# Scaling of the differential heads behind blocks of the first merge branch, and pending differential products ahead of the last latent transposes

## The chip, the cores and the metric

One Trainium2 chip, one of its cores. The metric is the device time of the whole program in microseconds (us). The program is built with a tile framework that plans the order of the instructions on each engine: it simulates the run, and whenever an engine is free it gives it the ready instruction that stands first in the program text. So an instruction may overtake earlier ones of its engine, unless the kernel ties it down. Once planned, the order on an engine is fixed, and the engine waits wherever a real transfer is later than the simulated one.

## The reference

Two layers of an encoder over 512 tokens and 1024 channels, all float32:

```python
for l in range(DEPTH):                       # DEPTH = 2
    h = _rmsnorm(x, g_mix_pre[l])
    z = h @ w_in[l]                          # latents, q/k/v of two branches, 3 gates
    o_a = _mla(c_q, c_kv, k_r, ...)          # 8 heads, low-rank q and kv, rotary part
    o_b = _dilated(...)                      # 4 heads, 3 strided groups, relative bias
    o_c = _diff(...)                         # 4 heads, two softmax maps, RMSNorm of each head
    gates = sigmoid(gz)
    merged = (gates[:, :, 0] * (o_a @ w_branch[l, 0]) + gates[:, :, 1] * (o_b @ w_branch[l, 1])
              + gates[:, :, 2] * (o_c @ w_branch[l, 2]))
    x = x + _rmsnorm(merged @ w_out[l], g_mix_post[l])
    x = x + _rmsnorm(relu(_rmsnorm(x, ..) @ w_up[l]) ** 2 @ w_down[l], ..)
```

The RMSNorm of a differential head divides its output by the root mean square over its 128 channels, token by token. The kernel calls this step the scaling of the head.

## The kernel before, in words

Every dense product is made of three float32r matmuls: operands are split into a high part (`whi`, `hhi`, a rounding copy on ACT) and a low part (`wlo`, `hlo`, a subtraction on DVE, or on POOL where the text says so). A weight block of 128 x 1024 is loaded on SP's queue into `wraw` (4 buffers), split, and used by `mm3` (L132).

A layer goes through these stages in the text:

- The opening of the first layer: `x` is loaded in four blocks of 128 tokens; `norm_scale` normalises a block, and `norm_turn` transposes it on TensorE (`ntp`, into `hhi` and `hlo`). `head_start` computes four products (`zq`) on the first two token blocks while blocks 2 and 3 are still being normalised by `start`, called through `turns`.
- Dilated heads (`dil_head`), differential heads (`diff_head`), latents (`latent`, `latent_turn`: products `cp`, transposes `ctp`), then eight latent heads (`mla_head`). A head works in four rounds of 128 queries. A round makes scores (`s`, `sd`, `ms`), a softmax on DVE, ACT and POOL, and puts its transposes (`tp`) and, every second round, its product with the values (`do`, `fo`, `mo`) on the list `pending`. `tick(2)` runs the entries more than two rounds old, and `drain()` runs all of them. In a product of a differential head, L679 adds the squares (`sp`), and `ond` and `rdr` in HBM receive the unscaled head and its reciprocal roots.
- `fill(n)` hands TensorE n units of the 24 gate products (`gp`). A unit is 6 matmuls and a gate has 4 units, so a layer has 96; fractions are carried over in `owed`. The argument is `RATES` per round, 1.5 in dilated, 2.0 in differential and 1.0 in latent heads, with 2.0 and 1.75 in the first two latent heads and `fill(2.0)` ahead of the last latent transposes. `fill(1000)` finishes the gates.
- The merge: for branch 1 (dilated), 2 (differential), 0 (latent), eight products `bp` of 12 matmuls each, two to a weight block; the loaded gate `gl` multiplies each, and DVE adds it to `macc`. `bp` has two PSUM buffers (tag `mm`), so a third product waits for the `macc` of the first. In branch 2, `diff_norm` loads a head and its factors (`dn<-ond`, `dn<-rdr`), multiplies them on DVE and splits the result into `ot` on ACT and DVE.
- Output projection (`e`), and the MLP (`up`, `p`, `e`).

`InOrder` wraps an engine: while `on`, each instruction is tied behind the one traced before it on its engine. Tiles of one tag share buffers: `se` (6) holds `em`, `dn` and `xn`; `pair` (13) holds the values and `ot`; `gt` (2) holds gates and `gl`. Before the change the opening is tied on ACT, DVE and SP until `head_start` has been traced in full. The POOL copies `wk` behind the latents are tied to the POOL instruction traced before them.

Of the kernel before, what the change touches and what calls it, by code (L numbers as in the profile page):

```python
# [26 lines left out]
RATES = (1.5, 2.0, 1.0)  # L27
# [39 lines left out]
class InOrder:  # L67


    def __init__(self, tc, eng):  # L70
        self.tc, self.eng, self.on = tc, eng, False

    def __getattr__(self, name):
        fn = getattr(self.eng, name)

        def call(*args, **kw):
            ins = fn(*args, **kw)  # L77
            if self.on:
                self.tc.keep_in_program_order(ins)
            return ins  # L80

        return call
# [8 lines left out]
def _trunk(ctx, tc, nc, a):  # L91
# [6 lines left out]
    def in_order(on, engines=(act, vec, sync)):  # L98
        for e in engines:
            e.on = on  # L100
# [10 lines left out]
    def pair(name, dt=F32R):  # L111

        t = sb.tile([128, 2, 512], dt, name=name, tag="pair", bufs=13)
        return t[:, 0], t[:, 1]
# [13 lines left out]
    def f(x):  # L128
        return x.bitcast(F32)
# [58 lines left out]
    def split_w(raw, cols=1024, eng=None):  # L188
        hi = sb.tile([128, 1024], F32R, name="whi", tag="whi", bufs=4)
        lo = sb.tile([128, 1024], F32R, name="wlo", tag="wlo", bufs=4)  # L190
        act.activation(hi[:, :cols], raw[:, :cols], AF.Copy)
        (eng or vec).tensor_tensor(lo[:, :cols], raw[:, :cols], f(hi)[:, :cols], op=OP.subtract)
        return hi, lo
# [188 lines left out]
    def by_chunk(t):  # L382

        return t.rearrange("p (j q) -> p q j", q=4)
# [39 lines left out]
    def chunked(t):  # L424
        return t.rearrange("p (c j) -> p c j", c=4)
# [45 lines left out]
    otd = {}  # L471
# [34 lines left out]
    def layer(l, h, first_w):  # L506
# [18 lines left out]
        def fill(n):  # L525
            owed[0] += n
            while owed[0] >= 1.0:
                owed[0] -= 1.0
                if next(gates, "end") == "end":
                    return  # L530
# [34 lines left out]
        def dil_head(hd, q, k, v, rate):  # L565
            b = hd % 2
            bt = biases.pop(0)
            ahead = None

            def product(half, pt):  # L570
                o = pst("do", "o", 256)
                for c in range(4):
                    cs = slice(hd * 128, hd * 128 + 128)
                    mm3(o, v[c][0][:, cs], v[c][1][:, cs], pt[0][:, c], pt[1][:, c], c == 0, c == 3)
                hi = tmp("doh", F32R)
                lo = tmp("dol", F32R)
                act.activation(hi[:, :256], o, AF.Copy)
                vec.tensor_tensor(lo[:, :256], o, f(hi)[:, :256], op=OP.subtract)
                store_ot(1, hd, half, hi, lo)

            pts = {}
            for r in range(4):
                half, i = r // 2, r % 2
                s0, s1 = pst("s0", "s"), pst("s1", "s", 256)
                score(s0, q[0], k[0], b, r * 128, 0, 512)
                score(s1[:, 0:128], q[1], k[1], b, r * 128, r * 128, 128)
                score(s1[:, 128:256], q[2], k[2], b, r * 128, r * 128, 128)
                s = se("sd", 768)
                m = small("dm", 4)
                vec.tensor_tensor_reduce(out=s[:, :512], in0=s0, in1=bt[:, (3 - r) * 128:(7 - r) * 128],  # L590
                                         scale=1.0, scalar=-3e38, op0=OP.add, op1=OP.max,
                                         accum_out=m[:, 0:1])
                vec.tensor_tensor_reduce(out=s[:, 512:], in0=s1, in1=bt[:, 896:], scale=1.0, scalar=-3e38,
                                         op0=OP.add, op1=OP.max, accum_out=m[:, 1:2])
                vec.tensor_scalar(m[:, 2:3], m[:, 0:1], m[:, 1:2], -0.125, op0=OP.max, op1=OP.mult)
                act.activation(s, s, AF.Exp, bias=m[:, 2:3], scale=0.125, accum_out=m[:, 3:4])
                rc = small("dr")
                vec.reciprocal(rc, m[:, 3:4])
                blk = s[:, r * 128:(r + 1) * 128]
                pool.tensor_tensor(s[:, 512:640], s[:, 512:640], s[:, 640:768], op=OP.add)  # L600
                pool.tensor_tensor(blk, blk, s[:, 512:640], op=OP.add)
                act.activation(s[:, :512], s[:, :512], AF.Copy, scale=rc)
                if hd < 3 and r == 0:
                    ahead = dil_bias(hd + 1)
                    biases.append(next(ahead))
                if hd < 3 and r == 2:
                    next(ahead)
                if l == 0 and r % 2:
                    next(evens, None)

                def flip_p(s=s, half=half, i=i):
                    if i == 0:
                        pts[half] = new_pt()
                    transpose_p(s, pts[half], i, flip)

                pending.append((flip_p, (lambda half=half: product(half, pts[half])) if i else None))
                tick(LAGS[0])
                fill(rate)

        first_bias = dil_bias(0)  # L620
        biases = [next(first_bias)]
# [152 lines left out]
        for c in range(4):  # L774
            z, zp = latent(c), z
            if c:
                latent_turn(c - 1, zp)
        fill(2.0)
        latent_turn(3, z)
        vec.tensor_tensor(kr[0:32], kr[0:32], krs[0:32], op=OP.add)  # L780
        qe = [sb.tile([128, 2, 512], F32R, name=f"q{e}", tag="pair", bufs=13) for e in range(2)]
# [130 lines left out]
            vm.append(row)  # L912
        for hp in range(4):
            hold = []
            mla_head(2 * hp, hold, RATES[2] if hp else 2.0)
            if hp < 3:
                place = mla_prep(hp + 1)
                place(0)
            mla_head(2 * hp + 1, hold, RATES[2] if hp else 1.75)
            if hp < 3:  # L920
                place(1)
# [1 line left out]
        fill(1000)  # L923


        def diff_norm(hd, out):

            t = se("dn", 1024)
            o, rb = t[:, :512], t[:, 512:]
            sync.dma_start(o, ond[hd])  # L930
            sync.dma_start(rb, bass.AP(tensor=rdr.tensor, offset=rdr.offset + hd * 512, ap=[[0, 128], [1, 512]]))
            vec.tensor_tensor(chunked(o), chunked(o), by_chunk(rb), op=OP.mult)
            act.activation(out[0], o, AF.Copy)
            vec.tensor_tensor(out[1], o, f(out[0]), op=OP.subtract)

        macc = [None] * 8
        mh, ml = [None] * 8, [None] * 8
        for bi, b in enumerate((1, 2, 0)):
            ot = [pair("ot") for _ in range(4)]
            for kc in range(4):  # L940
                if b == 2:
                    diff_norm(kc, ot[kc])
                    continue
                for j in range(2):
                    sync.dma_start(f(ot[kc][j]), otd[b][kc, j])
            for dp in range(4):
                w = weights(wi("w_branch")[b * 4 + dp])
                hi = w[0].rearrange("p (d k n) -> p d k n", d=2, k=4)
                lo = w[1].rearrange("p (d k n) -> p d k n", d=2, k=4)
                for d2 in range(2):  # L950
                    d = dp * 2 + d2
                    t = sb.tile([128, 512], F32, name="gl", tag="gt", bufs=2)
                    sync.dma_start(t, gated[b, d])
                    p = mmt("bp")
                    for k4 in range(4):
                        mm3(p, hi[:, d2, k4], lo[:, d2, k4], ot[k4][0], ot[k4][1], k4 == 0, k4 == 3)
                    if bi == 0:
                        if d2 == 0:
                            mt = sb.tile([128, 2, 512], F32, name="macc", tag="pt", bufs=4)
                        macc[d] = mt[:, d2]  # L960
                        vec.scalar_tensor_tensor(macc[d], t, 1.0, p, op0=OP.add, op1=OP.mult)
                    else:
                        vec.scalar_tensor_tensor(t, t, 1.0, p, op0=OP.add, op1=OP.mult)
                        vec.tensor_tensor(macc[d], macc[d], t, op=OP.add)
                    if bi == 2:
                        mh[d], ml[d] = pair("mrg")
                        act.activation(mh[d], macc[d], AF.Copy, scale=0.5)
                        vec.scalar_tensor_tensor(ml[d], macc[d], 0.5, f(mh[d]), op0=OP.mult, op1=OP.subtract)


        gpost = load_g(wi("g_mix_post"), "gpost")
# [212 lines left out]
        for qd in range(4):  # L1184
# [32 lines left out]
            last = l == DEPTH - 1  # L1217
# [24 lines left out]
    def start(c):  # L1242
        xns[c] = norm_scale(xs[c], g0)
        norm_turn(xns[c], c, h)
# [28 lines left out]
    ws = [split_w(raws[0], eng=pool)]  # L1273
    norm_turn(xns[1], 1, h)
    ws.append(split_w(raws[1]))
    for c in range(2, 4):
        turns[c] = lambda c=c: start(c)
    first = list(head_start(blocks, h, turns, "zq", ws))
    sync.dma_start(flip, a["flip"])
    in_order(False)  # L1280
    setup_bias()
    got = []
    def all_setup():
# [102 lines left out]
```

## Time and profile before

| | |
|---|---|
| median of 3 runs | 1871.1 us (1870.99 to 1872.38) |
| profiled execution | 1869.85 us, span 1868.1 us |
| granted TensorE clock, mean | 0.998 |
| TensorE matmul busy | 1820.8 us (97% of the span) |
| DVE, ACT, POOL busy | 67%, 51%, 27% |

The span is what the profiler saw between the first and last instruction; the execution's own time has 1.75 us around it. All times in rows count from the span's start. A matmul's end is modelled and overlaps the next one, so a stretch of matmuls is best read from start to start, or as a piece of the chain of work.

### The profile page before, as it was taken

The page shows a single profiled execution, that of the slowest core. Times are in us where ns is not written, and L with a number is a line of the kernel's source. Part 1 is how long each engine was busy: PE and PEld are TensorE (multiplying, and loading weights), DVE is VectorE, ACT ScalarE, POOL GpSimd, SP SyncE. Part 2 cuts the span into 40 slices and gives each one's busy share as a digit, 9 for nine tenths or more (in the row PEclk, how much of TensorE's full clock was granted, in tenths as well). Part 3 has the DMA queues.
Part 4 walks back from the last instruction along what each step waited for, and adds up shares of the span by engine and source line. Part 5 has one row for each costly group of instructions (what it writes and reads, how often), then busy time and mean ns, then how long its engine had stood idle before and what let it go on. Part 6 is the DMA issues. An engine that isn't in the chain of part 4 may idle for free.

```text
span 1868.1 us, 24762 instructions
## 1 busy us (share of the span) xinstructions
PE 1820.8 (97%) x9002; PEld 1523.6 (82%) x9002; DVE 1260.3 (67%) x2024; ACT 960.7 (51%) x1605; POOL 499.1 (27%) x367
## 2 busy tenths in 40 slices
PE   7999999999999999999999999999999999999998
PEld 6788788888777988788888887888887888878886
DVE  4855376656677786888674455675667779587965
ACT  4466355478525453443554554554783354543433
POOL 1344212331000242347123222114200015241542
PEclk9999999999999999999999999999999999999999
DMA  4365554346675432424453333544468562414243
GB/s 161 104 210 195 178 186 136 101 142 194 233 239 204 146 100 81 135 68 149 148 194 107 118 119 119 156 152 121 139 211 276 181 225 68 156 47 152 70 162 136
DMA packets 105843, 281.13 MB, mean 150 GB/s; under 512 B 13470, under 2 KB 19942, under 8 KB 105719
## 3 DMA queue, kind: packets, MB, share of 16 engines
q1 hardware_dynamic: 105718, 279.53, 46.0%
q8 instruction: 71, 1.16, 0.3%
q14 instruction: 54, 0.43, 0.1%
HBM read 228.50 MB, written 39.96 MB: 144 GB/s over the span
## 4 chain that ended last, share of the span: by engine, by line
PE 64%; DVE 10%; issue 4%; POOL 4%; DMA 3%; ACT 2%; SPq 0%; POOLq 0%; DVEq 0%; ACTq 0%
PE up L132 12%; PE gp L132 12%; PE p L132 9%; PE zq L132 7%; PE e L132 5%; PE bp L132 3%; DVE fr L77 3%; DVE wlo L77 3%; PE ms L132 2%; PE tp L465 2%; PE cp L132 2%; PE sd L132 2%; PE mo L132 1%; DVE fs L77 1%; POOL fr L77 1%
## 5 line engine op out<-in xcount | busy, mean ns | idle before, releaser
L77 ACT ACTIVATE whi<-wraw 128x1024 fp32r<-128x1024 f32 (+1 forms) x270 | 283.9, 1054 | 274.6 <-PE up L132 52.8
L77 DVE TENSOR_TENSOR wlo<-wraw,whi 128x1024 fp32r<-128x1024 f32 (+1 forms) x213 | 274.8, 1293 | 142.7 <-ACT whi L77 141.3
L77 POOL TENSOR_TENSOR wlo<-wraw,whi 128x1024 fp32r<-128x1024 f32 x57 | 139.3, 2447 | 369.5 <-ACT whi L77 369.5
L132 PE MATMUL up<-hlo,whi 128*128 128x512 f32 (+1 forms) x576 | 210.4, 366 | 0.0
L132 PE MATMUL up<-hhi,wlo 128*128 128x512 f32 (+1 forms) x576 | 210.4, 366 | 0.0
L132 PE MATMUL up<-hhi,whi 128*128 128x512 f32 (+1 forms) x576 | 209.9, 366 | 0.5 <-ACT hhi L77 0.5
L132 PE MATMUL p<-whi,fs 128*128 128x512 f32 x672 | 208.0, 389 | 0.0
L77 POOL TENSOR_TENSOR dw<-dw 128x1024 f32<-128x1024 f32 x48 | 132.1, 2755 | 144.6 <-DVE wlo L77 143.6
L132 PE MATMUL gp<-hhi,whi 128*128 128x512 f32 x384 | 153.0, 398 | 1.9 <-DVE ql L77 1.9
L132 PE MATMUL gp<-hhi,wlo 128*128 128x512 f32 x384 | 150.8, 393 | 0.3 <-POOL wlo L77 0.3
L132 PE MATMUL gp<-hlo,whi 128*128 128x512 f32 x384 | 150.3, 391 | 0.0
L132 PEld LDWEIGHTS p<-whi,fs 128*128 128x128 f32 x672 | 126.1, 188 | 26.1
L77 DVE TENSOR_TENSOR wlo<-dw,whi 128x1024 fp32r<-128x1024 f32 x84 | 138.0, 1662 | 13.7 <-POOL fr L77 10.9
L132 PE MATMUL zq<-hhi,whi 128*128 128x512 f32 (+1 forms) x384 | 138.7, 364 | 5.5 <-DVE ql L77 2.6
L132 PE MATMUL zq<-hhi,wlo 128*128 128x512 f32 (+1 forms) x384 | 138.7, 362 | 1.7 <-DVE wlo L77 1.0
L132 PE MATMUL zq<-hlo,whi 128*128 128x512 f32 (+1 forms) x384 | 138.3, 361 | 1.7 <-DVE hlo L77 1.7
L132 PE MATMUL p<-wlo,fs 128*128 128x512 f32 x336 | 131.5, 391 | 2.6 <-DVE wlo L77 2.6
L132 PE MATMUL bp<-ot,whi 128*128 128x512 f32 x384 | 120.3, 392 | 4.8 <-DVE macc L77 3.9
L77 ACT ACTIVATE whi<-dw 128x1024 fp32r<-128x1024 f32 x84 | 88.1, 1058 | 68.4 <-PE p L132 42.9
L132 PEld LDWEIGHTS up<-hlo,whi 128*128 128x128 f32 x576 | 108.6, 189 | 17.9 <-DVE hlo L77 0.4
L132 PEld LDWEIGHTS up<-hhi,whi 128*128 128x128 f32 x576 | 108.1, 188 | 18.4 <-ACT hhi L77 1.0
L132 PEld LDWEIGHTS up<-hhi,wlo 128*128 128x128 f32 x576 | 108.6, 189 | 17.5
(257 smaller groups left out, 4053.7 us busy)
## 6 DMA issues: line engine op xcount, KB each, us to landing
wraw<-in_w_up_dram SPq DMA_DIRECT2D x64, 512.0 KB, 4.3
wraw<-in_w_gate_dram SPq DMA_DIRECT2D x48, 512.0 KB, 3.7
dw<-in_w_down_dram SPq DMA_DIRECT2D x48, 512.0 KB, 3.4
btd<-ddram SPq DMA_DIRECT2D x64, 256.0 KB, 3.3
wraw<-in_w_out_dram SPq DMA_DIRECT2D x32, 512.0 KB, 3.4
wraw<-in_w_down_dram SPq DMA_DIRECT2D x32, 512.0 KB, 3.5
wraw<-in_w_dil_dram SPq DMA_DIRECT2D x24, 512.0 KB, 4.7
gated<-gt SPq DMA_DIRECT2D x48, 256.0 KB, 3.0
```

Of the source, the lines that this page charges most:

```text
L77: ins = fn(*args, **kw)
L132: pe.matmul(out, lhsT, rhs, start=first, stop=last)
L465: pe.transpose(p[:, k * 128:(k + 1) * 128], e[:, k * 128:(k + 1) * 128], perm)
```

## The change

Five edits. `InOrder` remembers its last tied instruction. In each first dilated head, rounds 0 and 1 get one gate unit more. The `fill(2.0)` ahead of the last latent transposes becomes `drain()`, and the first latent head gets 2.25 units per round. `diff_norm` becomes a generator: its loads are traced ahead of the weights of branch 1, and its arithmetic, tied on ACT and DVE, after each pair of blocks of that branch. In the opening, the tie ends ahead of `head_start`; only `start(2)` and `start(3)` are still queued behind the last tied instructions of ACT and DVE.

```diff
@@ InOrder
+                self.last = ins.ins
@@ dil_head
-                fill(rate)
+                fill(rate + (1.0 if hd == 0 and r < 2 else 0.0))
@@ ahead of the last latent transposes
-        fill(2.0)
+        drain()
         latent_turn(3, z)
@@ latent heads
-            mla_head(2 * hp, hold, RATES[2] if hp else 2.0)
+            mla_head(2 * hp, hold, RATES[2] if hp else 2.25)
@@ merge
-        def diff_norm(hd, out):
+        def diff_norm(hd):
             t = se("dn", 1024)
             o, rb = t[:, :512], t[:, 512:]
             sync.dma_start(o, ond[hd])
             sync.dma_start(rb, bass.AP(tensor=rdr.tensor, offset=rdr.offset + hd * 512, ap=[[0, 128], [1, 512]]))
+            yield
+            out = pair("ot")
+            in_order(True, [act, vec])
             vec.tensor_tensor(chunked(o), chunked(o), by_chunk(rb), op=OP.mult)
             act.activation(out[0], o, AF.Copy)
             vec.tensor_tensor(out[1], o, f(out[0]), op=OP.subtract)
+            in_order(False, [act, vec])
+            yield out
...
         for bi, b in enumerate((1, 2, 0)):
-            ot = [pair("ot") for _ in range(4)]
-            for kc in range(4):
-                if b == 2:
-                    diff_norm(kc, ot[kc])
-                    continue
-                for j in range(2):
-                    sync.dma_start(f(ot[kc][j]), otd[b][kc, j])
+            if b == 2:
+                ot = normed
+            else:
+                ot = [pair("ot") for _ in range(4)]
+                for kc in range(4):
+                    for j in range(2):
+                        sync.dma_start(f(ot[kc][j]), otd[b][kc, j])
+            if b == 1:
+                norms = [diff_norm(kc) for kc in range(4)]
+                for n in norms:
+                    next(n)
+                normed = []
             for dp in range(4):
...
+                if b == 1:
+                    normed.append(next(norms[dp]))
@@ opening
     ws.append(split_w(raws[1]))
+    last = [act.last, vec.last]
+    in_order(False)
+
+    def later(c):
+
+        with tc.issue_after(last[0]), tc.issue_after(last[1]):
+            start(c)
+
     for c in range(2, 4):
-        turns[c] = lambda c=c: start(c)
+        turns[c] = lambda c=c: later(c)
     first = list(head_start(blocks, h, turns, "zq", ws))
     sync.dma_start(flip, a["flip"])
-    in_order(False)
```

## Rows read from the trace of the kernel before

**Rows 1.** The page: each engine's busy time, share of the span, and instructions.

```profile
PE 1820.8 (97%) x9002; PEld 1523.6 (82%) x9002; DVE 1260.3 (67%) x2024; ACT 960.7 (51%) x1605; POOL 499.1 (27%) x367
```

**Rows 2.** Waits of TensorE: waiter, awaited, us in total, times, longest.

```profile
PE bp L132 <- DVE macc L77: 3.9, 2, 3.0
PE ctp L762 <- DVE zc L77: 3.2, 2, 1.6
```

**Rows 3.** Timeline of TensorE, opening: start, us, instruction, [idle before, releaser].

```profile
30.55 0.38 PE L132 MATMUL zq<-hhi,whi 128*128 128x256 f32 x1 [1.68 <-ACT whi L77]
...
31.81 0.38 PE L132 MATMUL zq<-hhi,wlo 128*128 128x256 f32 x1 [0.76 <-DVE nst L77]
```

**Rows 4.** Timeline of SP, DVE and ACT, opening.

```profile
5.47 1.17 SPq L77 DMA_DIRECT2D wraw<-in_w_dil_dram  x2
...
15.82 0.21 DVE L77 TENSOR_SCALAR gds<-cols 128x1 f32<-128x1 f32 x2 [2.72 <-DMA cols<-in_cols_dram]
...
29.44 1.06 ACT L77 ACTIVATE whi<-wraw 128x1024 fp32r<-128x1024 f32 x1
```

**Rows 5.** Timeline of POOL and TensorE, first dilated heads of both layers.

```profile
85.88 8.09 POOL L77 TENSOR_TENSOR wlo<-wraw,whi 128x1024 fp32r<-128x1024 f32 x3 [17.55 <-ACT whi L77]
...
95.72 0.66 PE L465 MATMUL tp<-flip,sd 128*128 128x128 f32 x4 [1.70 <-ACT sd L77]
...
1016.18 0.55 PE L465 MATMUL tp<-flip,sd 128*128 128x128 f32 x3 [0.84 <-ACT sd L77]
```

**Rows 6.** Timeline of all engines, last latent block, first layer.

```profile
356.57 1.61 POOL L77 CAST wk<-whi 128x512 fp32r<-128x512 f32 x1
...
357.25 0.20 ACT L77 ACTIVATION_READ_ACCUMULATOR zc<-cp 128x1 f32 x1
...
358.83 1.31 POOL L77 TENSOR_SCALAR csv<-cst 128x1 f32<-128x1 f32 x2
...
361.49 0.59 PE L762 MATMUL ctp<-ident,zc 128*128 128x128 f32 x3 [1.61 <-DVE zc L77]
```

**Rows 7.** Timeline of ACT and DVE, the latent block before it.

```profile
351.96 0.20 ACT L77 ACTIVATION_READ_ACCUMULATOR zc<-cp 128x1 f32 x1
...
353.27 0.74 DVE L77 TENSOR_SCALAR zc<-cp,csr 128x256 f32<-128x256 f32 x2 [2.25 <-POOL csr L77]
```

**Rows 8.** Chain of work: start, us, what; a gate stretch and a product.

```profile
373.38 2.75 PE gp L132 x12
...
380.21 1.42 PE fo L132 x12
```

**Rows 9.** Timeline of TensorE: one round's transposes.

```profile
335.75 0.60 PE L465 MATMUL tp<-flip,ed 128*128 128x128 f32 x4
```

**Rows 10.** Timeline of SP, DVE and TensorE, merge of the first layer.

```profile
492.83 0.43 SPq L77 DMA_DIRECT2D dn<-rdr  x1
...
505.11 1.06 DVE L77 TENSOR_TENSOR dn<-dn 128x512 f32<-128x512 f32 x1 [2.61 <-DMA dn<-rdr]
...
508.56 0.73 PE L132 MATMUL bp<-ot,whi 128*128 128x512 f32 x2 [2.99 <-DVE macc L77]
```

**Rows 11.** Chain of work, merges of both layers: start, us, what.

```profile
498.34 6.74 DMA dn<-rdr
...
1426.40 46.54 PE bp L132 x204
```

**Rows 12.** Groups by form, 488 to 532 us: count | busy, mean ns | idle before.

```profile
L77 DVE TENSOR_TENSOR wlo<-wraw,whi 128x1024 fp32r<-128x1024 f32 x6 | 7.3, 1217 | 0.2 <-ACT whi L77 0.2
L77 DVE SCALAR_TENSOR_TENSOR macc<-gl,bp 128x512 f32<-128x512 f32 x8 | 5.4, 683 | 3.7 <-PE bp L132 3.6
L77 DVE TENSOR_TENSOR dn<-dn 128x512 f32<-128x512 f32 x4 | 4.3, 1076 | 3.1 <-DMA dn<-rdr 3.1
...
L77 DVE TENSOR_TENSOR ot<-dn,ot 128x512 fp32r<-128x512 f32 x4 | 2.8, 690 | 0.8 <-ACT ot L77 0.7
L77 ACT ACTIVATE ot<-dn 128x512 fp32r<-128x512 f32 x4 | 2.5, 632 | 10.3 <-DVE dn L77 7.8 <-DMA dn<-ond 2.5
```

More of the change, by code (lines that the diff above doesn't have):

```diff
@@ L70, in __init__ @@
     def __init__(self, tc, eng):
-        self.tc, self.eng, self.on = tc, eng, False
+        self.tc, self.eng, self.on, self.last = tc, eng, False, None
     def __getattr__(self, name):
```

## The prediction

> **What bounds the kernel now.** I read the shares on the page first: TensorE is busy 97% of the span, DVE 67%, ACT 51%, POOL 27% [rows 1]. So the sum of the matmuls is the bound, and none of the five edits takes a matmul away. What can be won is TensorE's idle time, some 47 us by these shares. The second view is the list of what TensorE waited for, the third the timeline at each place that an edit touches: there the reader is to see which engine is late, and what stands ahead of the late instruction on it. Four places count. In the opening the products wait for a weight split and then for DVE [rows 3]. In the first dilated head the first transposes wait for ACT, in both layers [rows 5]. The last latent transposes wait for DVE, once in each layer [rows 2, 6]. In the merge a product waits for `macc`, twice in all [rows 2, 10].
>
> The measurement tells about 0.2% from no change, here 3.7 us.
>
> **The opening.** The weight block 3 is loaded early: SP issued blocks 2 and 3 at 5.47 [rows 4]. Its split on ACT runs only at 29.44 [rows 4], since it is tied behind the copies of `norm_turn(2)`, which stands before it in the text. TensorE waits 1.68 us for it, and 0.76 us more on DVE's queue, 2.44 together [rows 3]. With the tie gone, block 3 can be split while TensorE still works on block 2, and the norm of block 3 of `x` goes ahead of it too; `start(2)` and `start(3)` stay behind the last tied split. Bounds: 2.44 gained if both waits go; nothing if the planner leaves the order, or if the second norm's transposes meet a new wait as long as 0.76. I take 2.44 less 0.3.
>
> **The first dilated head.** At its third round TensorE has no more to do until the first softmax is scaled: 1.70 us in the first layer, 0.84 in the second [rows 5]. The edit puts two gate units, 12 matmuls, ahead of that point. Twelve take 2.75 us [rows 8], more than either wait, so 2.54 goes. No matmul is added: the units come out of later rounds. The cover needs the next gate's weights in time, and POOL, which splits them, also does this softmax's additions: three splits take 8.09 us, 2.70 each [rows 5]. One more split ahead of the additions would cost up to 2.70 a layer, the lower bound. The three already run before the additions and reach past the units now asked for, so I take 2.54.
>
> **The last latent transposes.** TensorE does two gate units and then waits 1.61 us; the list of waits has two such, 3.2 us [rows 2, 6]. The last square sum is ready at 357.45, but POOL turns to it at 358.83, being held by the copies `wk` that started at 356.57 [rows 6]. A block earlier the same chain ran from 352.16 to 354.01, 1.85 us [rows 7]. By that the last block would be ready at 359.30, some 2 us before 361.49. `drain()` does two things. It puts the two open rounds of the last differential head into the hole: two groups of transposes of at most 0.60 each and two products of 1.42, 4.04 us, and two short stretches of `sp`, where the 2.75 of gate work and the wait make 4.36 [rows 6, 8, 9]. And the last POOL instruction traced before `wk` is now the reciprocal root of that head, so `wk` is tied behind it and no longer runs ahead of the latent chain. What is late next is the second product: it needs its transposes copied by ACT and subtracted by DVE, which the latent chain uses too. Between its transposes and itself stand only 1.42 us of the other product. The loss is between nothing, if gate units or the latent transposes fill the gap, and all of 1.61 a layer. I take 0.4 a layer: 3.2 less 0.8. The work that leaves the first latent head, 4.04 us, is replaced there by one gate unit (2.25 in place of 2.0, 4 rounds) and, where that is not enough, by later units, which are ready.
>
> Gate units counted: 58 are asked for ahead of the latent heads before (24, 32, 2) and 58 after (26, 32, 0), but 40 in place of 39 in them. The last latent round but one thus loses its gate work, 1.37 us in each layer [rows 8]. Branch 1's products are loaded by then and independent, so I cost this at nothing; without that cover it is 1.37 a layer.
>
> **The merge.** In branch 2's scaling DVE stands 2.61 us at the last head's factors, and the `macc` of two finished products is queued behind it; TensorE, out of PSUM buffers, waits 2.99 [rows 10]. In the second layer the like costs 0.9, the rest of the 3.9 [rows 2, 10]. The load is not slow alone but late: SP issued it at 498.34, and it landed 6.74 us on [rows 11]. In the Trainium skill, the page "SBUF — State Buffer", in "The DMA setup-cost knee", gives a DMA some 2 us and its bytes at 436 GB/s, an estimate of 2.6 us for 256 KB. By that it would land at 500.9, DVE would not wait, and 2.99 of the sum would not be there to win; the row has 6.74, so the trace disagrees and decides.
>
> After the change the eight loads stand ahead of branch 1's weights in the text, and each head's scaling is tied behind the second `macc` of its pair of blocks. The first is needed after two products, the last after eight; `macc` no longer queues behind an unlanded load. DVE's work per pair of blocks: a weight split 1.22, two `macc` of 0.68, the scaling 1.08, ACT's copy 0.63, which DVE sits out, and the subtraction 0.69, together 4.98 us [rows 12]. TensorE needs 24 matmuls of 46.54/204 = 0.228, 5.47 [rows 11]. It fits with 0.49 to spare. At the border to branch 2 the last scaling comes out 0.68 + 1.08 + 0.63 + 0.69 = 3.08 us after the eighth product, and nine matmuls on the three other heads cover 2.05. The rest, 1.03 a layer, is the upper bound; nothing if the next product's nine go in between. I take 0.5 a layer: 3.9 less 1.0.
>
> **Sum.** 2.44 + 2.54 + 3.2 + 3.9 = 12.1 us removed; 0.3 + 0.8 + 1.0 = 2.1 given back; 10.0 net. The profiled execution of 1869.85 becomes 1859.9. The median of the runs shown stands 1.25 above it, so the prediction is 1861.
>
> **Rivals.**
>
> 1. The loads' wait moves instead of going. Eight loads at up to 0.43 of SP's time each [rows 10], 3.4 us, are now issued ahead of branch 1's weights and gates, and those start late: at worst 3.4 a layer, 6.8. Net 3.2, time 1868, within 0.2%. For it: SP's queue is in order, and landing takes up to 6.74 [rows 11]. Against it: before, loads of `dn` were also issued ahead of most `gl`, at 492.83 for one [rows 10], and TensorE did not stop for a gate.
>
> 2. The drained product is as late as the transposes were, and costs all of 3.2. Then 12.1 - 3.2 - 1.3 = 7.6, time 1863.5, still faster. For it: ACT and DVE serve both chains. Against it: the gate units are ready and planned into such gaps.
>
> 3. Slower: the opening. Without the tie, set-up work is planned ahead of splits and norms on DVE and ACT, and the plan takes its loads as landed sooner than they are. That exists now: DVE stood 2.72 us at `gds` for `cols` [rows 4]. The set-up has about ten such loads. At 2.72 each it takes four of them to eat the 10.0, and from the sixth on the kernel is slower beyond 0.2%: 16.3 - 10.0 = 6.3, time 1877. Against it: set-up stands behind the opening in the text, so it goes first only into time that the plan sees as idle.
>
> 4. The change doesn't do what it says: the planner gives the same orders, or TensorE's waits return a round later. Time 1871. Against it: the ties on ACT, DVE and POOL are edges that the planner can't ignore.
>
> **How the numbers follow.** My forecast 0.64, rival 2 0.14, rival 1 0.09, rival 3 0.07, rival 4 0.06. Faster is the forecast and rival 2, 0.78; same is rivals 1 and 4, 0.15; slower is rival 3, 0.07. The low end has nothing given back, 1871.1 - 12.1 = 1859, and one wait more that a new order may drop, as long as those of rows 3, 1857.3; I take 1857. The high end takes in rival 2 and rival 1 up to its 1868 with a little for the bound of POOL in the dilated head: 1869. Outside stay rivals 3 and 4.
>
> **What would show it.** Opening: the fourth split on ACT before 25 us, no wait over 0.5 after the transposes of `x` block 2. Dilated: no wait at the first `tp`. Latents: `fo` and `sp` between the last `cp` and the last `ctp`, `wk` after `csr`, no wait at `ctp`. Merge: each `dn` multiplication behind a `macc`, without a wait for a load, and no wait of `bp` for `macc`. Wrong would be: `gl` late in branch 1 (rival 1), a wait of `fo` for `ptl` (rival 2), DVE waiting for loads before 40 us (rival 3), or TensorE's idle sum unchanged (rival 4).

## The result, and the profile after

| | before | after |
|---|---|---|
| median | 1871.7 us (1870.99 to 1872.90) | 1897.8 us (1896.40 to 1900.17, 4 runs) |
| profiled execution | 1869.85 us, span 1868.1 us | 1896.40 us, span 1894.6 us |
| granted TensorE clock, mean | 0.998 | 0.993 |

The changed kernel is slower by 26 us: 1.014 times the time before, interval 1.0122 to 1.0158. The forecast was 1861, with a range of 1857 to 1869.

The page's shares of the changed kernel, to be held against [rows 1]:

```profile
PE 1834.4 (97%) x9002; PEld 1527.1 (81%) x9002; DVE 1254.4 (66%) x2024; ACT 959.1 (51%) x1605; POOL 491.3 (26%) x367
```

The same 9002 matmuls take 1834.4 us of busy time in place of 1820.8, and the span less the busy time is 60.2 us in place of 47.3. So half of the loss is TensorE waiting, and half is TensorE being busy for longer with the same work. The list of TensorE's waits (waiter, awaited, us in total, times, longest) names the first half:

```profile
PE s L133 <- DVE dm L77: 8.5, 4, 4.1
PE tp L466 <- ACT sd L77: 4.3, 5, 2.0
PE fo L133 <- DVE on L77: 4.0, 2, 2.0
...
PE zq L133 <- ACT gt L77: 2.6, 2, 1.3
...
PE vfp L133 <- POOL wlo L77: 2.0, 2, 1.0
PE vfp L133 <- ACT whi L77: 1.8, 2, 0.9
PE cp L133 <- ACT whi L77: 1.7, 2, 0.9
```

The waits that the change was aimed at [rows 2] are gone: no `ctp` on `zc`, no `bp` on `macc`. New ones stand in their place, and in stages in which the prediction had looked for none.

**The opening** is better. The two waits of [rows 3] are gone, and the first product of the dilated values starts at 61.46 in place of 65.27.

**The first dilated head** is worse. The timeline of POOL, ACT, DVE and TensorE:

```profile
82.06 9.45 POOL L77 TENSOR_TENSOR wlo<-wraw,whi 128x1024 fp32r<-128x1024 f32 x4 [17.55 <-ACT whi L77]
...
91.47 0.99 POOL L77 TENSOR_TENSOR sd<-sd 128x128 f32<-128x128 f32 x2
...
92.50 0.72 ACT L77 ACTIVATE sd<-sd,dr 128x512 f32<-128x512 f32 x1 [4.84 <-POOL sd L77]
...
95.25 0.72 ACT L77 ACTIVATE sd<-sd,dr 128x512 f32<-128x512 f32 x1 [1.11 <-POOL sd L77]
95.87 0.58 ACT L77 ACTIVATE gt<-gp 128x512 f32<-128x512 f32 x1
96.35 1.04 ACT L77 ACTIVATE whi<-wraw 128x1024 fp32r<-128x1024 f32 x1
...
97.48 1.23 DVE L77 TENSOR_TENSOR wlo<-wraw,whi 128x1024 fp32r<-128x1024 f32 x1 [3.15 <-ACT whi L77]
98.63 0.68 DVE L77 CUSTOM_DVE_ANT_0 sd<-s,bt 128x512 f32<-128x512 f32 x1
...
99.37 0.80 PE L133 MATMUL s<-ks,qs 128*128 128x512 f32 x1 [4.06 <-DVE dm L77]
```

Read it from the bottom. The scores of the fourth round wait 4.06 us for a PSUM buffer, which the bias sum of the third round (98.63) sets free. On DVE that sum stands behind a weight split (97.48), which waits 3.15 us for ACT's copy. On ACT the copy stands behind the gate's `gt` and behind the scaling of the second round's softmax (95.25), and that chain began late, at 92.50, behind four weight splits that POOL ran ahead of the first additions, where before it ran three [rows 5]. Whether that further split is the cause is asked below. In the second layer the same wait is 3.73.

**The borders between stages** have waits that none of the edits stands near. Between the dilated and the differential heads TensorE starts the products `vfp`, runs twelve gate matmuls in their midst, and then stops twice:

```profile
206.54 0.39 PE L133 MATMUL gp<-hhi,wlo 128*128 128x512 f32 x1
...
206.74 1.06 ACT L77 ACTIVATE whi<-wraw 128x1024 fp32r<-128x1024 f32 x1 [5.30 <-PE gp L133]
...
207.85 0.98 PE L133 MATMUL vfp<-whi,hhi 128*128 128x512 f32 x2 [0.92 <-ACT whi L77]
...
207.87 2.37 POOL L77 TENSOR_TENSOR wlo<-wraw,whi 128x1024 fp32r<-128x1024 f32 x1 [11.03 <-ACT whi L77]
...
210.29 0.59 PE L133 MATMUL vfp<-wlo,hhi 128*128 128x512 f32 x1 [0.99 <-POOL wlo L77]
...
296.67 0.60 ACT L77 ACTIVATE gt<-gp 128x512 f32<-128x512 f32 x1
...
297.32 0.50 PE L133 MATMUL zq<-hhi,whi 128*128 128x512 f32 x1 [1.28 <-ACT gt L77]
```

The row at 206.74 says it: a weight copy waits 5.30 us for a `gp`. A gate has four units. The two extra units leave a gate half done at this border, 26 units in place of 24 (and 14 in place of 12 between the two pairs of dilated heads). The open gate keeps its `whi` and `wlo`, and one of the two PSUM buffers of tag `mm`. The fourth weight block of `vfp` needs that `whi`. In the second pair of differential heads (the row at 297.32) a `zq` needs the PSUM buffer, and waits for ACT's `gt`.

**The last latents**: `wk` runs behind `csr` as forecast, but a gate's split takes its place ahead of the last chain on POOL, and the second drained product waits 2.02, longer than the 1.61 of the transposes before [rows 6].

```profile
375.54 2.43 POOL L77 TENSOR_TENSOR wlo<-wraw,whi 128x1024 fp32r<-128x1024 f32 x1 [3.47 <-ACT whi L77]
...
378.06 0.46 POOL L77 TENSOR_SCALAR csv<-cst 128x1 f32<-128x1 f32 x2
...
379.33 0.74 DVE L77 TENSOR_SCALAR zc<-cp,csr 128x256 f32<-128x256 f32 x2 [2.75 <-POOL csr L77]
...
381.04 0.48 DVE L77 TENSOR_SCALAR on<-fo,gds 128x256 f32<-128x256 f32 x1
...
381.58 0.39 PE L133 MATMUL fo<-pth,vf 128*128 128x256 f32 x1 [2.02 <-DVE on L77]
```

The second `fo` shares its PSUM tag (`o`) with the first `fo` and with `ctp`. DVE reads the first one (`on`, 381.04) only behind `zc`, and `zc` waits for POOL.

The second half of the loss stands in the windows (length, busy us of TensorE, of its weight loads, DVE, ACT, POOL, then the granted clock):

```profile
50.20:53.60 3.40, 3.08 (x9) 1.08 (x10) 2.51 (x5) 0.00 (x0) 0.58 (x1) 0.99 0.49 154
53.60:57.00 3.40, 3.40 (x9) 2.65 (x9) 1.90 (x2) 2.24 (x3) 0.00 (x0) 0.50 0.34 93
...
94.50:97.90 3.40, 0.81 (x4) 0.33 (x2) 0.42 (x1) 2.64 (x4) 0.63 (x2) 1.00 0.18 72
97.90:101.30 3.40, 1.93 (x7) 1.74 (x8) 3.15 (x9) 0.88 (x2) 0.00 (x0) 0.50 0.47 143
101.30:104.70 3.40, 3.40 (x12) 2.82 (x11) 0.90 (x7) 2.28 (x6) 3.09 (x4) 0.50 0.42 139
104.70:108.10 3.40, 3.40 (x24) 3.07 (x23) 1.98 (x4) 2.80 (x4) 2.25 (x3) 0.99 0.08 28
```

From 97.9, still within the 4.06 us wait, the clock stands at 0.50, 1.2 GHz in place of 2.4, for two of these stretches; in the stretch behind them TensorE has 24 matmuls, in the second at 0.50 it has 12, though not all of one size. The like is found at 196.9, 210.6 and 1036.6, behind a wait of `tp` (2.02), the two of `vfp`, and the `s` wait of the second layer. Ahead of the last matmuls there are six such stretches, 20.4 us, where before there were two, 6.8 us. At half the clock that is up to (20.4 - 6.8) / 2 = 6.8 us of the 13.6 of added busy time; the rest isn't accounted for by one cause.

### The profile page after: what moved, and what is told of

It is laid out like the page before. It is cut to its first block, busy times and chain, and to the rows that moved or that the text cites. A ratio compares the mean times of both kernels' runs of the same rounds, so it can differ in the third digit from the quotient of the medians.

```text
span 1894.6 us, 24762 instructions
## 1 busy us (share of the span) xinstructions
PE 1834.4 (97%) x9002; PEld 1527.1 (81%) x9002; DVE 1254.4 (66%) x2024; ACT 959.1 (51%) x1605; POOL 491.3 (26%) x367
## 5 line engine op out<-in xcount | busy, mean ns | idle before, releaser
L77 DVE TENSOR_TENSOR wlo<-wraw,whi 128x1024 fp32r<-128x1024 f32 (+1 forms) x213 | 267.9, 1261 | 163.1 <-ACT whi L77 162.6
L77 DVE TENSOR_TENSOR wlo<-dw,whi 128x1024 fp32r<-128x1024 f32 x84 | 138.1, 1663 | 13.7 <-POOL fr L77 10.9
```

## The experiments

Differences in us are taken to the median of the kernel before on the same chip: 1870.35 for the first four runs, 1871.52 for the next four, 1870.68 for the run with the units moved and the last two, 1869.83 for the rest. The first four and the opening alone ask which edit loses.

**The boost alone**

```diff
-                fill(rate)
+                fill(rate + (1.0 if hd == 0 and r < 2 else 0.0))
```

> The kernel before with one edit: one gate unit more in rounds 0 and 1 of the first dilated head. Theory (the boost is the cause: it brings a fifth weight split ahead of the softmax additions on POOL, and leaves a gate half done at each border of stages): 1888 to 1900 us, with the 4 us waits of the scores in both layers. Rival (the drain ahead of the latents is the cause, by the two 2.0 us waits of the last differential product and what follows): 1867 to 1873 us.

1895.6 us, +25.3, ratio 1.014 (1.0123 to 1.0157). The `s` waits of 4.06 and 3.74 and the waits of `vfp` and `zq` are all there, with a stretch of 3.4 us at half clock at each of the four places (the first was 6.8 in the changed kernel), and `ctp` waits 5.4 in place of 3.2. This line alone costs as much as the whole change.

**All but the boost** (the changed kernel with that line as before)

> The changed kernel without the boost; drain, scaling and opening stay. Theory (the boost is the cause): 1862 to 1870 us. Rival (the drain): 1885 to 1895 us.

1886.7 us, +16.4, ratio 1.0086 (1.0070 to 1.0103), in the range of the rival. So the other four edits lose too: the losses don't add up to the whole, they overlap. One loss that shows here is hidden in the changed kernel: `bp` waits 9.8 us for `macc`, in two waits, and there not at all.

**The drain alone** (with the 2.25)

```diff
-        fill(2.0)
+        drain()
         latent_turn(3, z)
...
-            mla_head(2 * hp, hold, RATES[2] if hp else 2.0)
+            mla_head(2 * hp, hold, RATES[2] if hp else 2.25)
```

> The kernel before with the drain ahead of the last latent transposes and 2.25 units in the first latent head. Theory (the boost is the cause; the drain only trades one wait for another): 1869 to 1875 us. Rival (the drain): 1885 to 1895 us.

1882.9 us, +12.5, ratio 1.0071 (1.0054 to 1.0088), between the two readings. `fo` waits 2.13 and 2.15, and there are two more waits further down, of `tq` (1.39, twice) and of `mo` (1.02, twice).

**Scaling and opening** (those two edits of the change, nothing else)

> The kernel before with the scaling behind the blocks of the first merge branch and the freed opening, nothing else. By the stretches of the two traces, the opening is worth 3.8 us and the merge 2.9 us together: 1863 to 1867 us under either theory. If these two edits too lose elsewhere what they win: 1869 to 1873 us.

1874.4 us, +4.0, ratio 1.0020 (1.0011 to 1.0030), above both readings. With the 12.5 of the drain that makes 16.5, the 16.4 of all but the boost.

**The opening alone**

> The kernel before with the edit of the opening alone (blocks 2 and 3 of x and of the weights untied from the written order, held behind two instructions only). The prediction's term: 2.1 gained. The changed kernel's trace had 3.8 gained by the first products of v. So 1866.5 to 1868.5, and the merge has its old waits near 2.99 and 0.9. The rival: what is gained is lost later by a shift against the loads or the clock, 1870.

1864.6 us, -6.9, ratio 0.9970 (0.9958 to 0.9981). By the difference of the two, the scaling costs 10.9 us. The opening wins three times what was forecast. The first product of the dilated values starts at 58.81, 6.46 earlier. The two waits of [rows 3] are 2.44 of that. By the clock's records the kernel before had two stretches at half clock between 30 and 60 us (at 32.7 and 56.6), which are not there now: 3.4 us. Only the first of them belongs to the edit: every run without the edit has a stretch between 31 and 37, at the two waits, and no run with it has one there. The second, behind set-up work, comes and goes with either opening (the changed kernel has it at 53.6). The merge's `macc` waits came down too, 3.9 in all to 2.4, though nothing was changed there, and a stretch at half clock came in at 183.9. So some 2.44 + 1.7 = 4.1 us is the edit's own, an estimate; the rest of the 6.9 came by chance with the new order.

The next four runs take the boost apart. The suspects are POOL's further split, the half-open gate, and the two early units themselves.

**Four units more instead of two**

```diff
-                fill(rate)
+                fill(rate + (2.0 if hd == 0 and r < 2 else 0.0))
```

> The kernel before with four more gate units in the first dilated head instead of two, so that the units asked for by the borders are 16, 28, 44, 60: a gate product is again just finished at each. POOL still has one weight split more ahead of the first softmax's additions. If the half-open gate at the borders is what costs: the first head's waits near 4 us stay, those of zq, vfp and ctp go, and the time is 1876 to 1881. If POOL's extra split and what follows from it is what costs: no better than the boost of two, 1892 or more.

1864.6 us, -6.9, ratio 0.9961 (0.9949 to 0.9974), better than either reading. Its timeline has POOL's four splits ahead of the additions as the changed kernel has:

```profile
86.52 9.45 POOL L77 TENSOR_TENSOR wlo<-wraw,whi 128x1024 fp32r<-128x1024 f32 x4 [19.06 <-ACT whi L77]
95.93 1.00 POOL L77 TENSOR_TENSOR sd<-sd 128x128 f32<-128x128 f32 x2
```

and yet no `s` waits over 0.3, and the transposes' 1.70 and 0.84 of [rows 5] are gone: 24 more matmuls cover the split. No `vfp` waits and no `zq` for `gt`. Between a gain of 6.9 and a loss of 25.3 stand two gate units per layer.

**Two units early, taken back in the same head**

```diff
-                fill(rate)
+                fill(rate + ((1.0 if r < 2 else -1.0) if hd == 0 else 0.0))
```

> The kernel before with one more unit in the first and second round of the first dilated head and one less in its third and fourth: the total is 12, 24, 40, 56 as before, and the order of POOL keeps four splits ahead of the first additions as before. If the two early units themselves were harmful, some of the 25 us shows, 1878 or more. If only the further split on POOL and the half-open gate are: no loss, and the term of the prediction shows, 2.5 gained, 1868 to 1870.

1880.0 us, +8.5, ratio 1.0042 (1.0028 to 1.0057). The first reading held: no border has a half-open gate here, POOL's order has no split more (three ahead of the first additions, as in [rows 5], and not four), and it still loses. The first head's timeline:

```profile
98.66 0.66 PE L465 MATMUL tp<-flip,sd 128*128 128x128 f32 x4 [1.29 <-ACT sd L77]
...
100.12 1.22 DVE L77 TENSOR_TENSOR wlo<-wraw,whi 128x1024 fp32r<-128x1024 f32 x1 [3.14 <-ACT whi L77]
...
102.01 0.80 PE L132 MATMUL s<-ks,qs 128*128 128x512 f32 x1 [2.70 <-DVE dm L77]
```

DVE's weight split ahead of the bias sum is late as in the changed kernel, and the units that would cover it were spent. The wait of 1.70 became 1.29 + 2.70, and around the second of them the clock stands at 0.50 for 6.8 us from 100.1; the second layer has the 2.70 too, with 3.4 us from 1025.1. So POOL's further split isn't needed for a wait like this.

**The two units late, in the second head**

```diff
-                fill(rate)
+                fill(rate + (1.0 if hd == 1 and r > 1 else 0.0))
```

> The kernel before with the two extra units in the third and fourth round of the second dilated head instead of the first two rounds of the first: TensorE has nothing more in front of the first transposes, but the total is 14, 26, 42, 58, and POOL's order has the further split ahead of the first additions. If the split on POOL makes the first head's waits of 4 us, they are there all the same. If the total does the rest, the time is that of the boost, 1890 to 1897; if the early units matter, it stays near 1875.

1891.2 us, +19.6, ratio 1.0104 (1.0087 to 1.0121). The border waits are those of the changed kernel. In the first head no `s` waits longer than 0.4; there POOL's split lengthens the transposes' wait from 1.70 to 3.05, and from 0.84 to 2.17 in the second layer, 2.7 together, and behind the 3.05 the clock stands at 0.50 for 3.4 us. The rest, some 15 us, comes behind the first head. This loss and the 8.5 of the run before make 28.1, near the 25.3 of the boost, which has both.

**The changed kernel with four units instead of two**

> The changed kernel with four units more in the first dilated head instead of two; nothing else differs. If the half-open gate at the borders makes the boost's loss here too, the waits of zq on gt and of vfp go and the time falls by some 20 us, to 1875 to 1881 (what drain and scaling cost by themselves stays). If the parts of the change only hurt together, it stays above 1890.

1869.8 us, 0.0, ratio 0.9999 (0.9989 to 1.0010). In the whole change too, a whole gate in place of half of one takes the loss away, all 26 us, more than the reading had. Two more units are also more cover; gate and cover are told apart by the two runs before this one, in which one of the two is as in the kernel before. `tq` has its 1.4 twice.

The drain was tested the same way.

**The drain with its units kept**

```diff
-        fill(2.0)
+        drain()
+        fill(2.0)
         latent_turn(3, z)
```

> The kernel before with the drained products ahead of the last latent transposes, but with the two gate units kept there too and the rate of the first latent head as before, so that all later borders stand at the same unit as before. If the drained product's own lateness costs (rival 2 of the prediction): the wait of fo stays near 2, and with it most of the 12.5 us of the run with the drain alone, 1880 or more. If the shifted units cost: tq's 1.39 and mo's 1.02 go, and the time is 1868 to 1873.

1870.6 us, +0.8, ratio 1.0003 (0.9993 to 1.0012). `tq` and `mo` don't wait as above. `fo` waits twice a layer, 0.60 and 1.09, together as long as the 1.61 of `ctp`: the wait has moved.

**The units moved, without the drain** (the `fill(2.0)` taken out, 2.25 in place of 2.0)

> The kernel before without the two gate units ahead of the last latent transposes and with 2.25 in place of 2.0 in the first latent head, but without the drained products: the units at the borders are those of the run with the drain (56 and 65 instead of 58 and 66). If the units cost by themselves, tq's wait near 1.39 and mo's near 1.0 appear, the wait of ctp grows from 1.6 by about the 2.75 us of work that is gone, and the time is 1877 to 1884. If the drain's order is needed for the loss, only the second shows: 1874 to 1876.

1879.2 us, +8.5, ratio 1.0045 (1.0028 to 1.0062). The list of waits:

```profile
PE ctp L762 <- DVE zc L77: 5.5, 2, 2.7
...
PE tq L132 <- DVE rt L77: 2.8, 2, 1.4
...
PE mo L132 <- DVE tq L77: 2.1, 2, 1.0
```

`tq` and `mo` wait without any drain. The timeline of ACT, POOL, DVE and TensorE at the first `tq` shows why:

```profile
423.11 1.06 ACT L77 ACTIVATE whi<-wraw 128x1024 fp32r<-128x1024 f32 x1 [0.70 <-issue]
...
424.25 2.40 POOL L77 TENSOR_TENSOR wlo<-wraw,whi 128x1024 fp32r<-128x1024 f32 x1 [9.46 <-ACT whi L77]
424.73 2.47 DVE L77 TENSOR_TENSOR mol<-ov,moh 128x512 fp32r<-128x512 f32 x1 [1.37 <-ACT moh L77]
427.12 0.68 DVE L77 TENSOR_TENSOR rt<-qr,cos_t 128x512 f32<-128x512 f32 x1
...
427.86 0.72 PE L132 MATMUL tq<-cq,whi 128*128 128x512 f32 x2 [1.40 <-DVE rt L77]
```

and in the kernel before:

```profile
420.75 0.69 DVE L77 TENSOR_TENSOR mol<-ov,moh 128x512 fp32r<-128x512 f32 x1 [0.51 <-ACT moh L77]
```

`tq` needs the PSUM buffer of `qr`, which `rt` reads. On DVE `rt` stands behind `mol`, the low part of a latent head's output. `mol` starts while POOL splits a gate's weights, ends 0.55 us after that split, and takes 2.47 us in place of 0.69. Before this `tq` TensorE has run 76 gate units here, with the drain alone and with all but the boost, and 80 in the changed kernel with four units: all four have a `mol` of 2.47 and the wait. With 77 (before, units kept), 78 (the changed kernel), 79 (the boost alone, units late) and 81 (four units alone) `mol` takes 0.69 and `tq` doesn't wait. 76 and 80 are whole gates, so the next gate's split comes just here. At this border the finished gate is the bad count.

**The scaling with two heads' loads ahead instead of four** (with the opening)

```diff
-                for n in norms:
+                for n in norms[:2]:
                     next(n)
...
                     normed.append(next(norms[dp]))
+                    if dp < 2:
+                        next(norms[dp + 2])
```

> Opening and scaling as in the run with both (1874.4), but only two heads' loads stand ahead of branch 1's blocks; the loads of the third and fourth head follow the first and second pair of blocks. On SP the second gate load comes after four loads of dn instead of eight. If the gate loads queued behind dn, and behind the stores that follow, are what costs (rival 1 of the prediction): the waits of bp near 3.29 and 2.59 go, and the time is 1863 to 1866, that of the opening alone or a little less. If the scaling's place on DVE is what costs: 1872 to 1875.

1864.0 us, -5.9, ratio 0.9966 (0.9954 to 0.9979): 10 us less than with all eight loads ahead, and no more than the opening alone. With all eight, SP, DVE and TensorE in the merge of the first layer:

```profile
484.75 0.41 SPq L77 DMA_DIRECT2D dn<-ond  x1
...
488.66 0.32 SPq L77 DMA_DIRECT2D dn<-rdr  x1
492.77 0.32 SPq L77 DMA_DIRECT2D ot<-moh  x1
493.50 0.32 SPq L77 DMA_DIRECT2D ot<-mol  x1
493.87 1.12 SPq L77 DMA_DIRECT2D gl<-gated  x2
...
497.63 0.69 DVE L77 SCALAR_TENSOR_TENSOR macc<-gl,bp 128x512 f32<-128x512 f32 x1 [2.68 <-DMA gl<-gated]
...
498.38 1.22 PE L133 MATMUL bp<-ot,whi 128*128 128x512 f32 x2 [3.29 <-DVE macc L77]
```

The eight loads end at 488.98. Then SP stands for 3.8 us at the store of the last latent head, whose data isn't there, and the second gate load is behind it, at 493.87. In the kernel before, three gate loads had gone out by 491.83, ahead of that store. With four loads, two gate loads get out ahead of that store (at 486.42 and 488.53), and `bp` waits 2.3 for `macc` in all in place of 6.4. The row of the 6.4, from the waits of the run with scaling and opening, and its windows behind the 3.29:

```profile
PE bp L133 <- DVE macc L77: 6.4, 3, 3.3
...
497.50:500.90 3.40, 2.52 (x6) 2.05 (x7) 2.97 (x4) 0.63 (x1) 0.00 (x0) 0.50 0.90 316
500.90:504.30 3.40, 3.40 (x9) 2.63 (x9) 0.00 (x0) 0.82 (x1) 0.00 (x0) 0.50 0.83 287
```

Around the 3.29 the clock stands at 0.50 for 6.8 us, which is up to 3.4 us more; with four loads there is no such stretch. The two make 7.5 of the 10.

**What won, put together.** Opening and four units:

> The kernel before with the opening and four more units in the first dilated head, the two edits that were faster by themselves (by 6.9 us each). If they win at different places: 1857 to 1860. If both won by a shift that takes the same wait in the merge (2.99 us) away: 1861 to 1864.

1860.3 us (1858.34 to 1861.95), -9.6, ratio 0.9944 (0.9928 to 0.9961), between the two readings and less than 6.9 twice: the `macc` waits, which went in part with the one and wholly with the other, can go only once.

All five edits, with four units, the drain's units kept, and two heads' loads ahead:

> All five edits, each without its side effect: four units more instead of two, the drain with its two gate units kept, the loads of two heads instead of four ahead of branch 1's blocks. If the prediction's gains are there once the side effects are gone, 1858 to 1861, at or below its 1861. If the drain gives nothing (its own run: no difference), the same as the run without it. If gains of one place overlap, 1862 to 1865.

1861.5 us, -9.2, ratio 0.9955 (0.9938 to 0.9971). The same without the drain:

> Opening, four units more, and the scaling with two heads' loads ahead; no drain. Opening and four units alone gave 1860.3. If the scaling adds a gain in the merge, 1856 to 1859; if the merge's waits were already gone by the other two edits, 1860 within 1.5.

1862.2 us, -8.5, ratio 0.9953 (0.9936 to 0.9969). The three can't be told apart. Without their side effects, drain and scaling are worth nothing that shows; the time forecast for the change, 1861, is what two of its ideas give, one of them with twice the units. That is chance and bears out none of the forecast's terms.

## Why the prediction was wrong

**The opening** was right in its mechanism and too small: 2.1 forecast, 6.9 measured. One term was missing, the stretch at half clock right behind the two waits, up to 1.7 us. The rest of the difference, the second stretch and a shift of the merge, is not the edit's and was luck.

**The dilated heads** hold the step that failed: "No matmul is added: the units come out of later rounds." The sum counted the units and not where the count stands at each border. Two units more leave a gate half done wherever a stage begins that needs its weight buffers or its PSUM buffer. With the units late, so that nothing but this and POOL's further split is left, it costs 19.6 us, some 15 of them behind the first head. The second part of the step, that 2.75 us of cover removes a wait of 1.70, failed as well: with two units moved inside the head the wait grew to 1.29 + 2.70, because behind the first wait the same chain on POOL, ACT and DVE is late once more. The price that the prediction named and did not take, a further split on POOL, came true at half its size: 1.35 us a layer where nothing covers it (four splits take 9.45 us where three took 8.09), nothing where four units do.

**The latents** failed at "replaced there by one gate unit", and at the gate work of which the prediction says "I cost this at nothing". The units moved cost 8.5 us without any drain. What they met is the split of the next gate on POOL, beside which `mol` takes 2.47 us on DVE, and a longer wait of `ctp`, 2.7. The drain's own effect has the size of rival 2, but not its mechanism: `fo` waits 2.0 in the changed kernel where `ctp` waited 1.6, and 0.60 + 1.09 with the units kept, not for its own transposes (`ptl`) but for a PSUM buffer that DVE reads late. With the units where they were, the drain gives nothing that shows.

**The merge** went by rival 1, which had a chance of 0.09 and a price of at most 6.8 us for both layers; the scaling cost 10.9. I had summed the loads' time on SP, 3.4 us, but not what stands behind them: a store that waits for a late engine, and the half clock around the wait that follows. The argument against this rival, that the loads of `dn` had stood ahead of gate loads before without harm, missed that three of the gate loads had left before the store. And the 3.9 us of `macc` waits weren't bound to the scaling: four units alone took them away, and the opening alone 1.5 of them.

**The rivals.** The slower side had 0.07, all on set-up loads in the opening, where nothing went wrong. Each of the three edits that lost does so by what it moves for others, and the prediction priced each only at its own place.

What stays open: about half of the added busy time isn't accounted for, and neither are some 3.5 of the 10.9 us of the scaling.

## What to carry to other kernels

When filler work comes in groups that hold buffers (a PSUM tile and a weight pair per four units here), an edit that moves some of it must keep the count at every later border where it was, or move whole groups: here two units cost 25 us and four won 7. Which count is good is a matter of the border: a finished gate was good ahead of the differential heads, and bad at the `tq` border, where the next gate's split then lands. Loads traced early on an in-order queue cost what the next blocked store on that queue makes of them, not their own issue time. A wait that ends is not yet won: look for the next wait of the same chain before putting it into a sum.

## What the runs showed of the hardware

A wait of TensorE can cost more than its length. In the changed kernel 6.8 us at a granted clock of 0.50 (1.2 GHz) began within a wait of 4.06 us, and 3.4 us each began within or up to 1.0 us behind waits of 2.02, 0.92 + 0.99 and 3.73. The Trainium skill, page "TensorE: Matmul & The Clock Gate", section "What's actually happening", has it that the slow state is the default and activity releases it; the windows agree, in that the full clock came back behind stretches filled with matmuls.

The same wait need not bring it. The `tp` at the end of the dilated heads waits 1.91 to 1.93 us in 14 of the 17 kernels run, the one before among them (at 188.11): in five a stretch of 3.4 us at 0.50 follows, in nine none does. It can also come without such a wait: at 50.2 to 53.6 in the changed kernel TensorE was busy 3.08 of 3.40 us, mostly with six set-up matmuls of 32 x 20 tiles, and the next stretch stood at 0.50; with the opening alone the same six, from 48.93, were followed by none. So what one trace shows of the half clock is in part luck.

A DVE subtraction can wait out a POOL instruction. `mol`, with both operands in SBUF, took 2.47 or 2.48 us each of the 14 times that it began during a weight split on POOL, and 0.67 to 0.69 in all other cases. DVE's `ptl`, which reads one operand from PSUM, took its 0.68 to 0.69 beside such splits too (20 times in the kernel before).
